# Key norms by products with a block of ones and ln/exp on channels, weight splits with a higher priority, and a new order of the first loads in a hybrid RWKV-7 / FoX block

## The chip, the core and the metric

The kernel runs on one core of a Trainium2 chip. A core has five engines, each with an instruction queue of its own that runs in order: TensorE (PE, matrix products and transposes into PSUM), VectorE (DVE), ScalarE (ACT, functions from tables and copies with a scale), GpSimd (POOL) and SyncE (SP, which here issues nearly all transfers). They wait for each other by semaphores. The metric is the device time of the kernel in microseconds; lower is better.

## The reference

One decoder layer in float32 over 272 tokens (16 meta tokens and 256 of the sequence), model width 2048, 16 heads of 64 in each of two branches, and a SwiGLU FFN of width 5632:

```python
xn = _rms(h, n1)
proj = xn @ w_in
z_rwkv, z_fox, z_gate = jnp.split(proj, (RWKV_COLS, RWKV_COLS + FOX_COLS), axis=-1)
...
# in _rwkv7
kk = heads((k * k_k).astype(F32))
kk = kk / jnp.maximum(jnp.sqrt(jnp.sum(kk * kk, axis=-1, keepdims=True)), 1e-12)
...
# in _fox
q = _rms(q.reshape(B, L, FOX_HEADS, HEAD_DIM), q_g)
k = _rms(k.reshape(B, L, FOX_HEADS, HEAD_DIM), k_g)
...
merged = g_a * (y_a @ w_a) + g_b * (y_b @ w_b)
h = h + merged @ w_o
gate, up = jnp.split(_rms(h, n2) @ w_gu, 2, axis=-1)
return h + (jax.nn.silu(gate) * up) @ w_dn
```

The change bears on the two norms over the 64 channels of a head, that of kk in `_rwkv7` and that of k in `_fox`, and on when things are done, not on what.

## The kernel before

**Layout.** Activations lie with channels on the partitions and tokens along the free dimension (128 x 272). Each large product is made of three float32r products: a weight tile `raw` (128 x 1024 float32) comes by a transfer on SP, ScalarE copies it to `wh` (rounded to float32r, L317), VectorE subtracts to get `wl` (L318), and x is held as the same kind of pair in `xhl`. There are three buffers each of raw, wh and wl. A tile serves one block of 16 to 32 matmuls (some 3 us on TensorE); its buffer is free for the third tile after it when the block's last matmul is done.

**Order of the work.** First come the lora products (`lora_jobs`, tiles `lo`), fed by `raw0` and x in pieces `xs`. The mean square of x is built beside them (`squares`, `rstd1`, tile `rms`), and `lora_post` makes the low rank inputs from them. Then, for each of four groups g of four heads: the products k, v, r and the low rank ones (`rwkv_jobs`), then the fox products q, k, v (`fox_jobs`, all tiles named `f`), then, in groups 0 to 2, two jobs of the gate product (`gate_jobs`, tiles `zg`, 256 columns each; the result of a job is copied out by ScalarE and completed by VectorE in `halves`, L393 and L394, and stored to memory as `zgd`). After group 3 the other gate jobs follow, then the branch products, w_o and the FFN.

**Small work.** What hangs on these products (the WKV recurrence in blocks, `rwkv_bg`; the attention, `fox_bg`; the norms) is written as generators. `slot` is called after every group of three matmuls, adds their time to a clock, and starts the next stage of a generator that is due. A stage yields the time until its next one: these are the constants at the head of the file (NORM, SUMS, Y_KK and the like). TensorE's order is so written out by hand (`manual_schedule`); in the lora part ScalarE's as well. The order on the other queues is made by a scheduler from priorities.

**The head norms before.** `head_sums` multiplies the squares (stationary, 128 channels x up to 128 tokens) with `bsum` (128 x 2), 4-byte float products: the sums of a head come out on token partitions, six products for 272 tokens and two tiles of channels (tiles `ss` for kk, `fss` for q and k). `rsqrt_steps` takes the inverse root there on VectorE with shifts and polynomials, and `spread` brings it back to channels: ScalarE widens it to 128 x 384 (L586) and TensorE transposes it, six transposes (tiles `kx` for kk, `fx` for the fox keys). VectorE multiplies (L679, L991).

**The softmax.** For each pair of heads `fox_bg` makes scores (`sc`), adds the bias of the forget gate with a row maximum, takes Exp on ScalarE with a sum (L1074), divides on VectorE (RECIPROCAL L1077, products L1081, tiles `s`) and transposes on TensorE (tile `ppt`), which ScalarE copies to `pT`; `po` is the product with v. Beside it VectorE runs a long chain of small steps for the inverse of the recurrence's triangular blocks (tiles `lx`, `lt`, L817 and L819).

Of the kernel before, what the change touches and what calls it, by code (L numbers as in the profile page):

```python
# [18 lines left out]
P = 128  # L19
# [47 lines left out]
STEP = 1000  # L67
NORM = 4200
SUMS = 2000
X_RS = 1400  # L70
X_SPREAD = 1400
X_V = 1900
# [4 lines left out]
Y_SQ = 1400  # L77
Y_SPREAD = 3300
Y_KK = 2900
Y_DECAY = 1400  # L80
Y_AB = 4400
Y_MAT = 2900
# [9 lines left out]
Y_GN = 1400  # L92
FORGET = 14000


@with_exitstack
def hybrid_block(ctx, tc, A, out, dbg=None):
# [70 lines left out]
    xh, xl = xhl[:, :, 0, :], xhl[:, :, 1, :]  # L168
    rsb = xp.tile([P, L], F32, tag="rsb", name="rsb")


# [63 lines left out]
    def xsplit(i, m):  # L235

        k, src = 2 * i + m, xs[i][:, m, :]
        nc.scalar.activation(xh[:, k, :], src, AF.Copy, scale=vc("n1", k))
        nc.vector.scalar_tensor_tensor(xl[:, k, :], src, vc("n1", k), xh[:, k, :].bitcast(F32),
                                       op0=ALU.mult, op1=ALU.subtract)  # L240

    def squares(i):

        if i == 0:
            nc.scalar.activation(xsum, xs[i], AF.Square)
# [24 lines left out]
    def rstd1():  # L270
        parts = [et(f"{n}1").bitcast(F32R) for n in ("xqh", "xql")]
        split(*parts, xsum)

        def back():
            ps = aux_ps("rms1")[:, :L]
            for i in range(4):
                nc.tensor.matmul(ps, allones, parts[i % 2][:, i // 2, :], start=i == 0, stop=i == 3)
            ms = zt_("ms1")[:, :L]
            nc.vector.tensor_scalar(ms, ps, 1.0 / D, RMS_EPS, op0=ALU.mult, op1=ALU.add)
            rt = zt_("rt1")[:, :L]  # L280
            rsqrt_small(None, rsb, ms, rt, None)
        return back
# [3 lines left out]

    zw = yb.rearrange("p g t -> p (g t)")[:, :T]
    nc.vector.memset(zw, 0.0)
    pz = aux_ps("warmup")[:, :T]
    for i in range(8):  # L290
        nc.tensor.matmul(pz, zw[:, :P], zw, start=True, stop=True)


    def wload(parts, n, between=None):
# [7 lines left out]
        for prow, c0, shape, srcs in parts:  # L302
# [13 lines left out]
            cs_ = slice(c0, c0 + size)  # L316
            nc.scalar.activation(wh[:prow, cs_], raw[:prow, cs_], AF.Copy)  # L317
            nc.vector.tensor_tensor(wl[:prow, cs_], raw[:prow, cs_], wh[:prow, cs_].bitcast(F32), op=ALU.subtract)  # L318
            res.append((v(wh), v(wl)))
# [152 lines left out]
    def lora_jobs():  # L472
        box = []

        def mk(q):
            def load():
# [18 lines left out]
            def mul(w):  # L495
                if q == 0:
                    box.extend((main_ps if i < 2 else aux_ps)(f"lo{i}") for i in range(4))
                pw, pa, pg0, pg1 = box[:4]
                wh, wl = w
                for k in range(2):  # L500
                    for ps, c0, m, n0, n in ((pw, 0, 96, 0, L), (pa, 96, 112, 0, L),
                                             (pg0, 208, P, 14, T + 2), (pg1, 208 + P, P, 14, T + 2)):
                        kt = q * 2 + k
                        mm3(ps[:m, :n], wh[:, k, c0:c0 + m], wl[:, k, c0:c0 + m],
                            xh[:, kt, n0:n0 + n], xl[:, kt, n0:n0 + n], kt == 0, kt == KT - 1)
# [8 lines left out]
        return [mk(q) for q in range(8)]  # L514

    def lora_post(pw, pa, pg0, pg1):
# [47 lines left out]

    def tiles(n):
        return [(n - T, P), (n - P, P)] + ([(0, NMETA)] if n > T else [])

    def head_sums(dst, sqs, n, name):  # L570


        ps = aux_ps(name)
        if n > T:
            nc.gpsimd.memset(dst, 1.0)
        for i, (t0, w) in enumerate(tiles(n)):
            for m in range(2):
                c = 4 * i + 2 * m
                pe_mm(ps[:w, c:c + 2], sqs[m][:, t0:t0 + w], bsum, start=True, stop=True)
        return [(dst[:w, 4 * i:4 * i + 4], ps[:w, 4 * i:4 * i + 4]) for i, (_, w) in enumerate(tiles(n))]  # L580

    def spread(rs, m, n, name):

        tl = tiles(n)
        ex = et(name).rearrange("p m t -> p (m t)")[:, :3 * P].rearrange("p (i c) -> p i c", c=P)
        nc.scalar.activation(ex[:, :len(tl), :].rearrange("p i (h d) -> p i h d", h=2),  # L586
                             rs.rearrange("p (i m h) -> p i m h", m=2, h=2)[:, :, m, :].unsqueeze(3).to_broadcast(
                                 [P, len(tl), 2, HD]), AF.Copy)

        def back():  # L590
            ps = aux_ps(name)[:, :n]
            for i, (t0, w) in enumerate(tl):
                pe_tr(ps[:, t0:t0 + w], ex[:w, i, :], ident[:w, :w])
            return ps
        return back

# [56 lines left out]
    def rwkv_bg(g, box):  # L653
# [16 lines left out]
        yield Y_SQ  # L670
        kn_ = rw.tile([P, 12], F32, tag="kn", name=f"kn{g}", bufs=2)
        kr_ = rw.tile([P, 12], F32, tag="kn", name=f"kr{g}", bufs=2)
        for d, ps in head_sums(kn_, [sq[:, m, :] for m in range(2)], L, f"ss{g}"):
            nc.vector.tensor_scalar(d, ps, 1e-24, None, op0=ALU.max)
        yield from rsqrt_steps(rw, kr_, kn_, [P, 12], "kt")
        backs = [spread(kr_, m, L, f"kx{g}{m}") for m in range(2)]
        yield Y_SPREAD
        for m in range(2):
            nc.vector.tensor_tensor(kk[:, m, :], kk[:, m, :], backs[m](), op=ALU.mult)  # L679
        yield Y_KK  # L680
# [281 lines left out]
    def fox_jobs(g):  # L962
# [5 lines left out]
        ready = []  # L968
        hs = fx.tile([P, 20], F32, tag="hs", name=f"hs{g}", bufs=4)
        hr = fx.tile([P, 20], F32, tag="hs", name=f"hr{g}", bufs=4)  # L970
        done = []

        def sums(sqs, dst, n):
            c = slice(0, 8) if dst is qn else slice(8, 20)
            for i, (d, ps) in enumerate(head_sums(hs[:, c], sqs, n, f"fss{g}{n}")):
                nc.vector.tensor_scalar(d, ps, 1.0 / HD, eps1[:d.shape[0], i:i + 1], op0=ALU.mult, op1=ALU.add)
            done.append(1)
            return
            yield

        def norms():
            while len(done) < 2:
                yield
            yield from rsqrt_steps(fx, hr, hs, [P, 20], "ht")
            yield X_RS

            nc.vector.tensor_tensor(hs[:, 0:8], hs[:, 0:8], hr[:, 0:8], op=ALU.mult)
            backs = [spread(hr[:, 8:20], m, L, f"fx{g}{m}") for m in range(2)]
            yield X_SPREAD
            for m in range(2):  # L990
                nc.vector.tensor_tensor(kn[:, m, :], kn[:, m, :], backs[m](), op=ALU.mult)  # L991
            yield
            ready.append(1)

        def post(dst, n):
            def f(pss):
                sqs = []
                for m in range(2):
                    ps = pss[m]
                    if dst is vv:  # L1000
                        nc.scalar.activation(dst[:, m, :], ps[:, :n], AF.Copy)
                        continue
                    sq = fx.tile([P, L], F32, tag="sqf", name=f"sqf{g}", bufs=3)
                    if dst is qn:
                        halves(dst[:, m, :], ps)
                        nc.scalar.activation(sq[:, :n], dst[:, m, :], AF.Square)
                    else:
                        nc.scalar.activation(sq[:, :n], ps[:, :n], AF.Square)
                        nc.scalar.activation(dst[:, m, :], ps[:, :n], AF.Copy, scale=qk8)
# [3 lines left out]
                else:  # L1013
                    spawn(sums(sqs, dst, n), SUMS)
                    if dst is kn:
                        spawn(norms(), PREP)
            return f
# [4 lines left out]
    def fox_bg(g, qn, kn, vv, hs, hr, ready):  # L1022
# [12 lines left out]
        yield  # L1035
        while not ready or not gate_done:
            yield X_V
# [72 lines left out]

    with tc.manual_schedule(engines={nc.scalar.engine}):

# [206 lines left out]
def _laid_out(inputs):  # L1319
# [30 lines left out]
    put("n2", a["norm2_g"][0])  # L1350
    return {"hT": hT, "lora": lora, "cols": cols}

# [20 lines left out]
```

## Time and profile before

| | |
|---|---|
| time, median of 3 runs | 1564.14 us (1563.58 to 1564.69) |
| profiled execution | 1564.61 us, of which span 1562.9 us |
| TensorE clock granted | 1.0 throughout |
| busy PE / DVE / ACT / POOL | 1554.3 / 1016.3 / 766.8 / 103.5 us |
| weight splits: wl on VectorE, wh on ScalarE | 605.2 us, 521.3 us (496 each) |
| loads of activation tables on ScalarE | 14, 1.283 us each |
| start of the first lora product, of the first k product | 6.84 us, 32.72 us |

Rows of the timeline give start and length in us, engine, line, operation and "out<-in" by the program's names; in brackets stands how long the engine was idle before and who released it. Rows of the waits give the waiting engine and line, whom it waited for, and the sum, the number and the longest of the waits. A row of windows gives for a stretch the busy time (and number) of PE, PEld, DVE, ACT and POOL, then the granted clock, the share of the DMA engines and GB/s.

### The profile page before, as it was taken

What the parts mean: (1) busy time and instruction counts of PE and PEld (TensorE: products, weight loads), DVE (VectorE), ACT (ScalarE), POOL (GpSimd) and SP (SyncE); (2) the same over time, 40 slices, a digit from 0 to 9 for tenths busy, and PEclk for the clock granted to TensorE, in tenths of its full rate; (3) what the DMA queues carried; (4) which work ended last, traced back from release to release, by engine and by line L of the source; (5) the groups of instructions that cost most, each with busy time, mean ns of one, the idle gap of its engine ahead of it and who ended that gap; (6) DMA issues with size and microseconds to landing.
All of it is one profiled execution on the core that took longest, in us unless ns stands there. A gap on an engine that the chain in (4) does not pass through costs nothing.

```text
span 1562.9 us, 26174 instructions
## 1 busy us (share of the span) xinstructions
PE 1554.3 (99%) x10227; PEld 1366.6 (87%) x10227; DVE 1016.3 (65%) x1854; ACT 766.8 (49%) x1117; POOL 103.5 (7%) x194
## 2 busy tenths in 40 slices
PE   9999999999999999999999999999999999999998
PEld 8999988989889888999888888888888888888887
DVE  8878688677768856875655666566566656444443
ACT  6655455465445544654444554454445544333332
POOL 2121103102203100000000000000000000000000
PEclk9999999999999999999999999999999999999999
DMA  7656546546545566776666666666666666666664
GB/s 238 177 155 173 158 125 180 157 119 168 166 137 146 166 179 190 248 226 225 190 183 181 186 186 190 189 188 188 189 189 188 185 193 187 187 203 198 188 200 131
DMA packets 211483, 283.33 MB, mean 181 GB/s; under 512 B 23888, under 2 KB 128352, under 8 KB 211360
## 3 DMA queue, kind: packets, MB, share of 16 engines
q1 hardware_dynamic: 206752, 277.43, 60.3%
q10 hardware_dynamic: 4608, 4.23, 0.8%
q8 instruction: 80, 1.31, 0.4%
q14 instruction: 43, 0.35, 0.1%
HBM read 274.43 MB, written 7.19 MB: 180 GB/s over the span
## 4 chain that ended last, share of the span: by engine, by line
PE 95%; DVE 2%; DMA 1%; issue 1%; ACT 1%; SPq 0%; ACTq 0%; DVEq 0%; POOL 0%
PE up L387 10%; PE gt L387 10%; PE zg L387 7%; PE dn L1238 5%; PE dn L1237 5%; PE dn L1236 5%; PE up L389 5%; PE gt L389 5%; PE zg L389 3%; PE f L328 2%; PE f L387 2%; PE f L330 2%; PE f L329 2%; PE br L329 2%; PE br L330 2%; PE br L328 2%
## 5 line engine op out<-in xcount | busy, mean ns | idle before, releaser
L318 DVE TENSOR_TENSOR wl<-raw,wh 128x1024 fp32r<-128x1024 f32 (+1 forms) x496 | 605.2, 1221 | 438.7 <-ACT wh L317 437.7
L317 ACT ACTIVATE wh<-raw 128x1024 fp32r<-128x1024 f32 (+1 forms) x496 | 521.3, 1052 | 628.7 <-PE dn L1237 146.3
L387 PE MATMUL gt<-hts,wh 128*128 128x512 f32 x704 | 245.0, 394 | 0.0
L387 PE MATMUL up<-hts,wh 128*128 128x512 f32 x704 | 244.9, 394 | 0.0
L389 PE MATMUL gt<-hts,wl 128*128 128x256 f32 x660 | 186.2, 282 | 0.0
L389 PE MATMUL up<-hts,wl 128*128 128x256 f32 x660 | 186.0, 282 | 0.0
L387 PE MATMUL zg<-xhl,wh 128*128 128x512 f32 x512 | 184.3, 403 | 0.0
L387 PEld LDWEIGHTS up<-hts,wh 128*128 128x128 f32 x704 | 130.1, 188 | 26.5
L387 PEld LDWEIGHTS gt<-hts,wh 128*128 128x128 f32 x704 | 130.1, 188 | 26.4
L1237 PE MATMUL dn<-wh,acl 128*128 128x512 f32 x352 | 139.5, 396 | 0.0
L1236 PE MATMUL dn<-wh,ach 128*128 128x512 f32 x352 | 139.5, 396 | 0.0
L1238 PE MATMUL dn<-wl,ach 128*128 128x512 f32 x352 | 139.5, 396 | 0.0
L389 PE MATMUL zg<-xhl,wl 128*128 128x256 f32 x480 | 135.0, 281 | 0.0
L389 PEld LDWEIGHTS up<-hts,wl 128*128 128x128 f32 x660 | 124.7, 189 | 1.8
L389 PEld LDWEIGHTS gt<-hts,wl 128*128 128x128 f32 x660 | 124.7, 189 | 1.8
L387 PEld LDWEIGHTS zg<-xhl,wh 128*128 128x128 f32 x512 | 94.6, 188 | 20.9 <-issue 1.8
L389 PEld LDWEIGHTS zg<-xhl,wl 128*128 128x128 f32 x480 | 90.6, 189 | 1.1
L1238 PEld LDWEIGHTS dn<-wl,ach 128*128 128x128 f32 x352 | 66.3, 188 | 16.2
L1237 PEld LDWEIGHTS dn<-wh,acl 128*128 128x128 f32 x352 | 66.3, 188 | 16.2
L1236 PEld LDWEIGHTS dn<-wh,ach 128*128 128x128 f32 x352 | 66.3, 188 | 16.1
L328 PE MATMUL f<-xhl,wh 128*128 128x272 f32 x256 | 77.7, 303 | 0.0
L330 PE MATMUL f<-xhl,wl 128*128 128x272 f32 x256 | 73.8, 288 | 0.0
(452 smaller groups left out, 2783.3 us busy)
## 6 DMA issues: line engine op xcount, KB each, us to landing
raw<-in_w_gate_up_dram SPq DMA_DIRECT2D x176, 512.0 KB, 3.8
raw<-in_w_in_dram SPq DMA_DIRECT2D x160, 512.0 KB, 4.1
raw<-in_w_down_dram SPq DMA_DIRECT2D x88, 512.0 KB, 4.7
raw<-in_w_o_dram SPq DMA_DIRECT2D x32, 512.0 KB, 4.3
raw<-in_w_branch_a_dram SPq DMA_DIRECT2D x16, 512.0 KB, 4.4
raw<-in_w_branch_b_dram SPq DMA_DIRECT2D x16, 512.0 KB, 4.8
zgd<-zg ACTq DMA_DIRECT2D x30, 128.0 KB, 2.4
gate<-zgd SPq DMA_DIRECT2D x15, 256.0 KB, 5.6
```

The lines of the kernel that those rows point to most:

```text
L317: nc.scalar.activation(wh[:prow, cs_], raw[:prow, cs_], AF.Copy)
L318: nc.vector.tensor_tensor(wl[:prow, cs_], raw[:prow, cs_], wh[:prow, cs_].bitcast(F32), op=ALU.subtract)
L328: nc.tensor.matmul(ps, wh, ah, start=first, stop=False)
L329: nc.tensor.matmul(ps, wh, al, start=False, stop=False)
L330: nc.tensor.matmul(ps, wl, ah, start=False, stop=last)
L387: nc.tensor.matmul(ps.rearrange("p (a t) -> p a t", a=2), wh, act, start=first, stop=last)
L389: nc.tensor.matmul(ps[:, :T], wl, act[:, 0, :], start=False, stop=False)
L1236: nc.tensor.matmul(box[t], ah[:, kt, ts_], wh[:, k, :], start=first, stop=False)
L1237: nc.tensor.matmul(box[t], al[:, kt, ts_], wh[:, k, :], start=False, stop=False)
L1238: nc.tensor.matmul(box[t], ah[:, kt, ts_], wl[:, k, :], start=False, stop=last)
```

## The change

**Key norms.** kk and the fox keys no longer go over token partitions. `head_norms` splits the squares into a float32r pair and multiplies each half with `bones` (128 x 128, ones in the two blocks of 64): the sum of a head stands at once on each of its channels, over 272 columns; two products for each of two tiles of channels (tiles `ss` and `fk`). The inverse root follows on channels: Ln, then Exp with scale -0.5, then Square on ScalarE, and a correcting step with three operations on VectorE. The query norm stays on token partitions (`q_norms`, 8 columns). The fox keys' root has its tile in the same buffer (tag "bias") as the bias of the attention.

**Splits.** In `wload` both split instructions are issued with a priority that is 200 higher.

**First loads.** The first lora weights come in two pieces at the head of SP's queue, x's first tile with its scale as an extra column on ScalarE's queue, and the other pieces of x one load later than before; the first tile's products run in another order; the warmup shrinks from 8 products of 256 columns to 7 of 128; the mean square of x is used in a stage that is due 2.5 us after the lora products (`token_scales`) rather than at once; VectorE's order too is written by hand in this part. Some of the constants are new.

```diff
-NORM = 4200
-SUMS = 2000
-X_RS = 1400
-X_SPREAD = 1400
+NORM = 6500
+SUMS = 3500
...
+N_SUM = 2000
+N_ROOT = 3600
...
-Y_AB = 4400
+Y_AB = 6000
...
+AHEAD = 200
+SCALES = 2500
...
+    epsw = xp.tile([P, L], F32, tag="epsw", name="epsw")
...
     raw0 = wp.tile([P, 1024], F32, tag="raw", name="raw", bufs=RAWB)
+    x0 = zt_("x0")[:, :L + 1]
     xs[0] = et("xs0")
-    nc.sync.dma_start(xs[0][:, 0], A["hT"][:, 0])
-    nc.scalar.dma_start(raw0[:, :NLO], A["lora"][0][:, :NLO])
+    nc.sync.dma_start(raw0[:, :NLO], A["lora"][0][:, :NLO])
+    nc.scalar.dma_start(x0, A["hT0"])
+    nc.sync.dma_start(raw0[:, NLO:2 * NLO], A["lora"][0][:, NLO:])
+    nc.scalar.dma_start(vcol, A["cols"])
     nc.sync.dma_start(xs[0][:, 1], A["hT"][:, 1])
-    nc.scalar.dma_start(vcol, A["cols"])
-    nc.sync.dma_start(raw0[:, NLO:2 * NLO], A["lora"][0][:, NLO:])
     xload(1)
...
-    zw = yb.rearrange("p g t -> p (g t)")[:, :T]
+    zw = yb.rearrange("p g t -> p (g t)")[:, :P]
...
-    for i in range(8):
-        nc.tensor.matmul(pz, zw[:, :P], zw, start=True, stop=True)
+    for i in range(7):
+        nc.tensor.matmul(pz, zw, zw, start=True, stop=True)
...
-            nc.scalar.activation(wh[:prow, cs_], raw[:prow, cs_], AF.Copy)
-            nc.vector.tensor_tensor(wl[:prow, cs_], raw[:prow, cs_], wh[:prow, cs_].bitcast(F32), op=ALU.subtract)
+            with tc.high_priority(AHEAD):
+                nc.scalar.activation(wh[:prow, cs_], raw[:prow, cs_], AF.Copy)
+                nc.vector.tensor_tensor(wl[:prow, cs_], raw[:prow, cs_], wh[:prow, cs_].bitcast(F32), op=ALU.subtract)
...
-                if q + 2 < 8:
-                    xload(q + 2)
+                if 0 < q < 7:
+                    xload(q + 1)
...
-                    box.pop()()
-                    lora_post(*box)
-                    spawn(forget_gate(), FORGET)
+                    spawn(token_scales(*box), SCALES)
...
+    def head_norms(xs, root, dst, floor, name):
+        parts = []
+        for m in range(2):
+            hi, lo_ = (zt_(f"{n}{name}{m}")[:, :L].bitcast(F32R) for n in ("nh", "nl"))
+            split(hi, lo_, xs[m])
+            parts.append((hi, lo_))
+        yield N_SUM
+        pss = []
+        for m in range(2):
+            ps = aux_ps(f"{name}{m}")[:, :L]
+            for i, part in enumerate(parts[m]):
+                clock[2] += L / 2.4
+                nc.tensor.matmul(ps, bones, part, start=i == 0, stop=i == 1)
+            pss.append(ps)
+        for m in range(2):
+            floor(xs[m], pss[m])
+        ys = root()
+        zs = [zt_(f"nz{name}{m}")[:, :L] for m in range(2)]
+        for m in range(2):
+            nc.scalar.activation(ys[m], xs[m], AF.Ln)
+        for m in range(2):
+            nc.scalar.activation(ys[m], ys[m], AF.Exp, scale=-0.5)
+        for m in range(2):
+            nc.scalar.activation(zs[m], ys[m], AF.Square)
+        yield N_ROOT
+        for m in range(2):
+            nc.vector.tensor_tensor(xs[m], xs[m], zs[m], op=ALU.mult)
+            nc.vector.scalar_tensor_tensor(ys[m], xs[m], -3.0, ys[m], op0=ALU.add, op1=ALU.mult)
+            nc.vector.scalar_tensor_tensor(dst[:, m, :], ys[m], -0.5, dst[:, m, :], op0=ALU.mult, op1=ALU.mult)
...
+        yield from head_norms([sq[:, m, :] for m in range(2)], root, kk,
+                              lambda x_, ps: nc.vector.tensor_scalar(x_, ps, 1e-24, None, op0=ALU.max), f"ss{g}")
...
+        def k_norms(sqs):
+            def root():
+                y = fx.tile([P, 2, L], F32, tag="bias", name=f"fy{g}", bufs=1)
+                return [y[:, m, :] for m in range(2)]
+            yield from head_norms(sqs, root, kn,
+                                  lambda x_, ps: nc.vector.scalar_tensor_tensor(
+                                      x_, ps, 1.0 / HD, epsw, op0=ALU.mult, op1=ALU.add), f"fk{g}")
+            ready.append(1)
...
-    with tc.manual_schedule(engines={nc.scalar.engine}):
+    with tc.manual_schedule(engines={nc.scalar.engine, nc.vector.engine}):
```

The scheduler's order follows, at three places. Lines are those of the kernel in question; in the changed one they are 10 to 28 higher.

VectorE in group 0, at the division of the softmax of the first pair of heads (`s_164` to `s_167` before, `s_165` to `s_168` after; `zg_0_1781` and `zg_0_1768` are the first half of the same gate job). Before:

```order
L1077 RECIPROCAL sums_1848<-sums_1848 128x4
L819 TENSOR_TENSOR lx_1665<-lx_1665,lt_1666 112x6x16
L1081 TENSOR_SCALAR s_164<-s_164,sums_1848 128x144
L817 TENSOR_TENSOR lt_1666<-lx_1665,ln_1476 112x6x15
L1081 TENSOR_SCALAR s_166<-s_166,sums_1848 128x144
L819 TENSOR_TENSOR lx_1665<-lx_1665,lt_1666 112x6x15
L1081 TENSOR_SCALAR s_165<-s_165,sums_1848 128x272
L817 TENSOR_TENSOR lt_1666<-lx_1665,ln_1476 112x6x14
L1081 TENSOR_SCALAR s_167<-s_167,sums_1848 128x272
L819 TENSOR_TENSOR lx_1665<-lx_1665,lt_1666 112x6x14
L394 TENSOR_TENSOR zg<-zg,zg_0_1781 128x256
```

And after:

```order
L328 TENSOR_TENSOR wl<-raw,wh 128x1024
L847 TENSOR_TENSOR lx_1695<-lx_1695,lt_1696 112x7x13
L1100 RECIPROCAL sums_1820<-sums_1820 128x4
L404 TENSOR_TENSOR zg<-zg,zg_0_1768 128x256
L845 TENSOR_TENSOR lt_1696<-lx_1695,ln_1508 112x7x12
L1104 TENSOR_SCALAR s_165<-s_165,sums_1820 128x144
L847 TENSOR_TENSOR lx_1695<-lx_1695,lt_1696 112x7x12
L1104 TENSOR_SCALAR s_167<-s_167,sums_1820 128x144
L845 TENSOR_TENSOR lt_1696<-lx_1695,ln_1508 112x7x11
L1104 TENSOR_SCALAR s_166<-s_166,sums_1820 128x272
L847 TENSOR_TENSOR lx_1695<-lx_1695,lt_1696 112x7x11
L1104 TENSOR_SCALAR s_168<-s_168,sums_1820 128x272
```

The gate's addition moved from behind the four divisions to ahead of the first, and a weight split, which waits for the end of the gate job's third block, to ahead of RECIPROCAL.

ScalarE in group 0, from the end of the first gate job (halves `zg_0` and `zg_1`) to the first exponential. Before:

```order
L317 ACTIVATE wh<-raw 128x1024
L393 ACTIVATE zg<-zg_0_1595 128x256
L317 ACTIVATE wh<-raw 128x1024
L393 ACTIVATE zg<-zg_1_1596 128x256
L1138 DMA zgd<-zg 128x256
L317 ACTIVATE wh<-raw 128x1024
L1138 DMA zgd<-zg 128x256
L317 ACTIVATE wh<-raw 128x1024
L1074 ACTIVATE s_164,sums_1848<-s_164,nm_1855,hr_997 128x144
```

And after:

```order
L830 ACTIVATE BK_1593<-tr_1661 128x2x2x64
L832 ACTIVATE SV_1594<-tr_1661 16x2x2x64
L403 ACTIVATE zg<-zg_0_1587 128x256
L1161 DMA zgd<-zg 128x256
L327 ACTIVATE wh<-raw 128x1024
L403 ACTIVATE zg<-zg_1_1588 128x256
L327 ACTIVATE wh<-raw 128x1024 x2
L1161 DMA zgd<-zg 128x256
L327 ACTIVATE wh<-raw 128x1024
L1097 ACTIVATE s_165,sums_1820<-s_165,nm_1827,hr_1000 128x144
```

The same four splits are in both. The first of them, the one that the next gate job begins with, stood ahead of the copy of `zg_0` and now stands behind it and behind its store.

ScalarE in group 1, between two weight splits, where the fox keys' root is taken. This piece is new (before, two copies of L586 stand there, with no load of a table):

```order
L327 ACTIVATE wh<-raw 128x1024
L618 ACT_TABLE_LOAD
L618 ACTIVATE fy_3124<-sqf_2991 128x272
L620 ACT_TABLE_LOAD
L620 ACTIVATE fy_3124<-fy_3124 128x272
L622 ACTIVATE nzfk_3125<-fy_3124 128x272
L618 ACT_TABLE_LOAD
L618 ACTIVATE fy_3124<-sqf_2994 128x272
L620 ACT_TABLE_LOAD
L620 ACTIVATE fy_3124<-fy_3124 128x272
L327 ACTIVATE wh<-raw 128x1024
L622 ACTIVATE nzfk_3126<-fy_3124 128x272
```

Two channel tiles take Ln and Exp in turn, and a table is loaded ahead of each of the four. In the whole program these loads rise from 14 to 34; TensorE's matmuls fall from 9517 to 9452.

More of the change, by code (lines that the diff above doesn't have):

```diff
@@ L244, in squares @@
         if i == 0:
-            nc.scalar.activation(xsum, xs[i], AF.Square)
+            for m, src in enumerate((x0[:, :L], xs[0][:, 1, :])):
+                nc.scalar.activation(xsum[:, m, :], src, AF.Square)
             return
@@ L563, in forget_gate, with head_sums @@
         gate_done.append(1)
-    def tiles(n):
-        return [(n - T, P), (n - P, P)] + ([(0, NMETA)] if n > T else [])
-    def head_sums(dst, sqs, n, name):
+    def head_sums(dst, sqs, name):
         ps = aux_ps(name)
-        if n > T:
-            nc.gpsimd.memset(dst, 1.0)
-        for i, (t0, w) in enumerate(tiles(n)):
+        for i in range(2):
             for m in range(2):
                 c = 4 * i + 2 * m
-                pe_mm(ps[:w, c:c + 2], sqs[m][:, t0:t0 + w], bsum, start=True, stop=True)
-        return [(dst[:w, 4 * i:4 * i + 4], ps[:w, 4 * i:4 * i + 4]) for i, (_, w) in enumerate(tiles(n))]
@@ L582, in spread @@
[L582 to L595, printed above, removed]
+                pe_mm(ps[:, c:c + 2], sqs[m][:, i * P:(i + 1) * P], bsum, start=True, stop=True)
@@ new lines, in head_sums @@
+        return [(dst[:, 4 * i:4 * i + 4], ps[:, 4 * i:4 * i + 4]) for i in range(2)]
+    def head_norms(xs, root, dst, floor, name):
[27 more added lines that the diff above has]
+            nc.vector.scalar_tensor_tensor(dst[:, m, :], ys[m], -0.5, dst[:, m, :], op0=ALU.mult, op1=ALU.mult)
@@ L670, in rwkv_bg @@
         yield Y_SQ
[L671 to L679, printed above, removed]
+        def root():
+            y = et(f"ny{g}")
+            return [y[:, m, :] for m in range(2)]
+        yield from head_norms([sq[:, m, :] for m in range(2)], root, kk,
+                              lambda x_, ps: nc.vector.tensor_scalar(x_, ps, 1e-24, None, op0=ALU.max), f"ss{g}")
         yield Y_KK
@@ L968, in fox_jobs, with sqf, q_norms, root @@
         ready = []
[L969 to L992, printed above, removed]
+        hs = fx.tile([P, 8], F32, tag="hs", name=f"hs{g}", bufs=4)
+        hr = fx.tile([P, 8], F32, tag="hs", name=f"hr{g}", bufs=4)
+        def sqf(m):
+            return fx.tile([P, L], F32, tag="sqf", name=f"sqf{g}{m}", bufs=3)
+        def q_norms(sqs):
+            for i, (d, ps) in enumerate(head_sums(hs, sqs, f"fss{g}")):
+                nc.vector.tensor_scalar(d, ps, 1.0 / HD, eps1[:, i:i + 1], op0=ALU.mult, op1=ALU.add)
+            yield from rsqrt_steps(fx, hr, hs, [P, 8], "ht")
+            nc.vector.tensor_tensor(hs, hs, hr, op=ALU.mult)
+            ready.append(1)
+        def k_norms(sqs):
+            def root():
+                y = fx.tile([P, 2, L], F32, tag="bias", name=f"fy{g}", bufs=1)
+                return [y[:, m, :] for m in range(2)]
+            yield from head_norms(sqs, root, kn,
+                                  lambda x_, ps: nc.vector.scalar_tensor_tensor(
+                                      x_, ps, 1.0 / HD, epsw, op0=ALU.mult, op1=ALU.add), f"fk{g}")
             ready.append(1)
@@ L1002, in f @@
                         continue
-                    sq = fx.tile([P, L], F32, tag="sqf", name=f"sqf{g}", bufs=3)
+                    sq = sqf(m)
                     if dst is qn:
@@ L1035, in fox_bg @@
         yield
-        while not ready or not gate_done:
+        while len(ready) < 2 or not gate_done:
             yield X_V
```

40 lines of the change are left out of this document (26 added, 14 removed).

## The prediction, made before the changed kernel was run

> **What bounds the kernel now.** I read the page's busy shares and its chain first, then the waits of TensorE, then the timeline at the places that the change touches.
>
> ```profile
> PE 1554.3 (99%) x10227; PEld 1366.6 (87%) x10227; DVE 1016.3 (65%) x1854; ACT 766.8 (49%) x1117; POOL 103.5 (7%) x194
> ...
> PE 95%; DVE 2%; DMA 1%; issue 1%; ACT 1%; SPq 0%; ACTq 0%; DVEq 0%; POOL 0%
> ...
> PE po L350 <- ACT pT L1093: 1.5, 1, 1.5
> PE warmup L291 <- DVE yb L288: 1.2, 1, 1.2
> PE rms L277 <- DVE xql L455: 0.9, 1, 0.9
> PE ppt L354 <- DVE s L1081: 0.6, 2, 0.3
> PE rms L277 <- ACT xqh L454: 0.3, 1, 0.3
> ...
> 45.00:610.00 565.00, 562.93 (x4735) 507.41 (x4734) 421.99 (x1054) 294.01 (x493) 94.66 (x148) 1.00 0.56 158
> ```
>
> TensorE is busy for 99% of the span and its listed waits add up to 4.5 us. So the time falls by what TensorE no longer does, and rises by every wait that it gets; there is little old waiting to win. The last row is the stretch that the change reorders (45 to 610 us; columns PE, PEld, DVE, ACT, POOL): VectorE works 422 of 565 us there, ScalarE 294. They keep up on average; what counts is whether, at one place, their queues hand TensorE its operand late. The sum is made against the profiled execution: 1564.61 us, 1562.9 of it span. The median of the three runs is 1564.14, 0.5 lower, inside their spread.
>
> **TensorE work removed and added.** One group of heads (g = 0) in the timeline of PE:
>
> ```profile
> 77.63 1.15 PE L350 MATMUL ss<-bsum,sq 128*128 128x2 f32 x12
> 78.71 0.50 PE L387 MATMUL f<-xhl,wh 128*128 128x512 f32 x1
> ...
> 85.56 1.07 PE L354 MATMUL kx<-ident,kx 128*128 128x128 f32 x6
> 86.56 0.39 PE L328 MATMUL f<-xhl,wh 128*128 128x272 f32 x1
> ...
> 102.03 1.13 PE L350 MATMUL fss<-bsum,sqf 128*128 128x2 f32 x12
> 103.09 0.39 PE L328 MATMUL f<-xhl,wh 128*128 128x272 f32 x1
> ...
> 115.76 1.07 PE L354 MATMUL fx<-ident,fx 128*128 128x128 f32 x6
> 116.76 0.50 PE L387 MATMUL zg<-xhl,wh 128*128 128x512 f32 x1
> ...
> 111.84 0.28 PE L772 MATMUL bs<-rkh,bones 128*128 128x256 f32 x1
> 112.31 0.29 PE L328 MATMUL f<-xhl,wh 128*128 128x272 f32 x1
> ```
>
> From the start of each piece to the start of what follows: 1.08, 1.00, 1.06 and 1.00 us. The product behind each takes another 0.10 longer than its like (0.50 for the first zg after fx against 0.39, the rate it has elsewhere). That is 4.54 a group, 18.2 for four. In their place come eight float32r products with `bones` a group, 272 columns wide. Four of 256 columns (bs) take 0.47, so four of 272 about 0.50: 1.0 a group, 4.0 in all. Net **-14.2**. The query sums stay.
>
> **The first microseconds.**
>
> ```profile
> 1.24 5.95 PE L291 MATMUL warmup<-yb 128*128 128x256 f32 x16 [1.24 <-DVE yb L288]
> 6.84 0.47 PE L328 MATMUL lo<-xhl,wh 128*96 128x272 f32 x1
> ...
> 30.43 0.28 PE L330 MATMUL lo<-xhl,wl 128*128 128x258 f32 x1
> 32.72 0.29 PE L328 MATMUL k<-xhl,wh 128*128 128x272 f32 x1
> ...
> 3.88 0.67 DVE L487 CAST wh<-raw 128x464 fp32r<-128x464 f32 x1 [2.70 <-DMA raw<-in_lora_dram]
> ...
> 8.52 0.59 ACT L490 ACTIVATE wh<-raw 128x464 fp32r<-128x464 f32 x1 [1.42 <-DMA raw<-in_lora_dram]
> ```
>
> The warmup shrinks to 7 products of half the columns (5.95 x 7/16 = 2.6, done near 3.9), and x comes with its own scale column; what is left is the cast of the first weights, done at 4.55. So the first lora product may start near 4.6 instead of 6.84. The 24 products of its tile take 3 us (0.125 each), and then the second tile is needed, whose split began at 8.52 on a landing. TensorE came there at 9.85; now it waits until about 9.0. I take **-0.9**; the ends are 0 (the landing moves later) and 2.3 (it moves earlier by as much as the first product). The statistics of the first norm (rms) leave the gap ahead of k: 2.29 from the last lora product's start to k's, less 0.12 for that product and 0.5 for the four sums, which stay: **-1.7**; k's first products need weights that are split long before. The two old waits of ppt, 0.6 in the rows above, are within the new ones below and fall as gains: **-0.6**. Gains: 14.2 + 0.9 + 1.7 + 0.6 = 17.4; 20.3 if the landing comes early and the 1.5 of po (a late load) goes as well.
>
> **The softmax transposes (ppt).** Before, VectorE divides s as soon as the sums are there; now a weight split and the gate's addition stand ahead of it.
>
> ```profile
> 139.18 0.60 ACT L1074 ACTIVATE s<-s,nm,hr 128x272 f32<-128x272 f32 x1
> 139.78 1.04 ACT L317 ACTIVATE wh<-raw 128x1024 fp32r<-128x1024 f32 x1
> ...
> 139.91 0.18 DVE L1077 RECIPROCAL sums<-sums 128x4 f32<-128x4 f32 x1
> 140.15 0.29 DVE L1081 TENSOR_SCALAR s<-s,sums 128x144 f32<-128x144 f32 x1
> 140.88 0.36 DVE L1081 TENSOR_SCALAR s<-s,sums 128x272 f32<-128x272 f32 x1
> 142.23 1.23 DVE L318 TENSOR_TENSOR wl<-raw,wh 128x1024 fp32r<-128x1024 f32 x1
> ...
> 139.55 0.39 PE L387 MATMUL zg<-xhl,wh 128*128 128x512 f32 x1
> 139.90 0.40 PE L387 MATMUL zg<-xhl,wh 128*128 128x512 f32 x1
> ```
>
> The split's buffers are freed by the third weight block of the gate product (here the fourth begins at 139.90). From there: wh 1.04 on ScalarE, wl 1.23 on VectorE, then, by the spacing of the rows (139.91 to 140.15 with one lx step between), lx 0.15, RECIPROCAL 0.15, the gate's addition 0.34 (0.42 alone, row below), lt 0.16, the first division 0.29: ready 3.4 after the block's end. TensorE needs only the half block before ppt: four pairs of 0.35 (139.55 to 139.90), 1.4. The operand of the second transposes comes 0.7 behind the first, and their work covers some of it. So at least 2.65 late in each of four groups; behind ppt stand the rest of the gate's block and, on ScalarE, the copies of ppt and of the gate's second half, which come later by as much. With the last exponential, now behind wh (0.60), and one more split (1.23) in the way it would be 4.5. I take 3.2, near the lower end, whose rows are all above: **+12.8** (10.6 to 18).
>
> **The switch from one gate job to the next.** (zg of one column block to zg of the next, one switch in each group.) Before, the next job's first wh is split ahead of the copies of the job that ends (zg halves); now behind the first of them, and in group 0 also behind its store, which waits for VectorE's addition.
>
> ```profile
> 128.91 0.38 ACT L393 ACTIVATE zg<-zg 128x256 f32<-128x256 f32 x1 [3.32 <-PE zg L387]
> 129.19 1.05 ACT L317 ACTIVATE wh<-raw 128x1024 fp32r<-128x1024 f32 x1
> ...
> 129.33 0.42 DVE L394 TENSOR_TENSOR zg<-zg,zg 128x256 f32<-128x256 f32 x1 [1.09 <-ACT zg L393]
> 130.28 1.22 DVE L318 TENSOR_TENSOR wl<-raw,wh 128x1024 fp32r<-128x1024 f32 x1 [0.39 <-ACT wh L317]
> ```
>
> From the first copy: 0.28 to the start of wh, 1.05, 0.05, 1.22 for wl: 2.6, and 0.3 of lx steps; TensorE has 1.4 less 0.15 of other work until the first product with wl. So 1.65 late, and in group 0 (addition 0.42, DMA issue) 2.15: **+7.1** for four. Low end 3.6 (0.9 each, wh alone late), high 8.5.
>
> **ScalarE's tables.** A group had 2 loads of tables and has 7 now; four of them stand in one piece between two weight splits (Ln, Exp, square, Ln, Exp of the fox keys). Before, a load lies between a split and an Ln so:
>
> ```profile
> 54.93 1.06 ACT L317 ACTIVATE wh<-raw 128x1024 fp32r<-128x1024 f32 x1
> 56.01 1.28 ACT L538 ACT_TABLE_LOAD   x1
> 57.30 0.43 ACT L538 ACTIVATE fa<-fa 16x272 f32<-16x272 f32 x1
> ```
>
> Four loads of 1.28 and five operations of 0.43 less what they overlap are some 7.1 us; the next split, and the copies of yT behind it, wait for them. In groups 1 to 3 a transpose (trbk) needs the PSUM of yT: I get 1.1 to 1.85 there, hence **+4.5** (0 if ScalarE comes early, 5.5). Group 0 has no yT. [...]
>
> **Two smaller ones.** In group 0 the bk of mat stands behind a split that waits for a block's end: 1.05 + 1.22 and about 1.6 of bk and its neighbours, less twelve products (1.5): **+2.4** (1.5 to 3). The query sums stand behind a wh: 0.55 once and 0.15 three times, **+1.0** (0 to 1.6). The bk row:
>
> ```profile
> 96.17 0.69 DVE L703 TENSOR_TENSOR bk<-kf,cs 128x512 f32<-128x512 f32 x1
> ```
>
> Queues: on SP the bias loads now wait for the key norm (one buffer for both), with the weight loads of the gate behind them; the loads of X are one weight load further forward. Covered by three raw tiles as far as I can follow, so 0; uncovered it costs the 1.5 of po each time, up to 6.5 in four groups. What comes after the last gate product is the same program in the same order: 0.
>
> Sum: 1564.6 - 17.4 + 12.8 + 7.1 + 4.5 + 2.4 + 1.0 = **1575.0**. With all low ends of the waits (15.7) and the high end of the gains: 1564.6 - 20.3 + 15.7 = 1560.0; with all high ends (36.6) and no gain at the first loads: 1564.6 - 16.5 + 36.6 = 1584.7.
>
> **Rivals.**
> - *The splits are one block further ahead than I read* (faster). There are three buffers of wh and wl. If the split ahead of RECIPROCAL, and the one behind the gate's copies, serve one block later than I take them for, their buffers are free 2.8 us (one block) earlier, more than the 2.65 of ppt and the 1.65 of the switch. Then only the two smaller terms stay: 1564.6 - 17.4 + 3.4 = 1550.6. For it: wh at 129.19 stands behind a copy too, and TensorE does not wait. Against: the waits in the changed program name the third block. 18 in 100.
> - *The loops are half as long*: the engines start up to 0.1 before the end of the last operation, and lateness at one place gives the next a lead. Half of 27.8: 1564.6 - 17.4 + 13.9 = 1561.1. 12 in 100.
> - *Loads late*: SP held by the bias, +6.5 to +8: about 1582. 10 in 100.
> - *A switch of tables costs as much again as its row*: four more of 1.28 in each of three groups, 15.4 us: 1590. Against it stands the Ln that starts 1.29 after its load. 3 in 100. [...]
>
> **How the numbers follow.** Forecast 1575, 57 in 100, its own range 1560 to 1585. About 0.2% (3 us) is what a measurement can tell from no change. Faster: the first rival 18, most of the second 9, and 3 from the forecast's low end: 30. Same: 3 of the second and 4 of the low end: 7. Slower: 63. The range runs from the first rival's 1550.6, rounded down, to late loads with high ends, 1588; outside it I leave half of the first rival, the fourth, and a tail of the third, 17 in 100.
>
> **What would show it.** PE's waits by line: ppt on a division in four groups, 2.6 to 4.5 each; the first zg product of four jobs on wl (or wh), 1.6 to 2.2; trbk in groups 1 to 3 on yT; mat once. ss and fk at 0.5 for four. ScalarE's loads at 1.28 with the next operation directly behind. First lora product near 4.6, no wait of rms. If ppt and zg wait less than 1 us in all, the forecast falls and the time is near 1550. If TensorE's small work costs other than 14.2 less, the first term is wrong.

## The result and the profile after

The changed kernel takes 1592.99 us (median of 4 runs, 1591.42 to 1594.66), the kernel before beside it 1564.41 (4 runs, 1563.58 to 1564.76): ratio 1.0181, 95% interval 1.0169 to 1.0194. It is slower, by 28.6 us. The forecast was slower by 10 and the range ended at 1588: the sign was right, the size wrong. Three executions in the experiments (one each of e1, e2 and e12) took 2496 to 3882 us and are in no median below; the medians of 1562.4 (e1) and 1592.5 (e2) from which later expectations start still count them.

The profiled execution took 1592.48 us, 27.9 more than that of before. First the page, then TensorE's waits (engine, line, whom it waited for; sum, number and longest, us):

```profile
span 1590.8 us, 26044 instructions
...
PE 1551.8 (98%) x10113; PEld 1360.3 (86%) x10113; DVE 1037.7 (65%) x1859; ACT 803.1 (50%) x1186; POOL 91.2 (6%) x186
...
PE 85%; DVE 6%; ACT 2%; DMA 1%; issue 1%; ACTq 0%
...
PE trbk L364 <- ACT ya L970: 8.3, 3, 2.8
PE ppt L364 <- DVE lt L845: 8.2, 3, 2.8
PE zg L399 <- DVE wl L328: 5.7, 5, 1.3
PE ppt L364 <- DVE s L1104: 3.5, 4, 2.7
PE mat L360 <- DVE bk L731: 2.0, 1, 2.0
PE fss L360 <- ACT sqf L1031: 1.5, 1, 1.5
PE v L338 <- DVE fl L546: 1.1, 1, 1.1
...
PE zg L397 <- ACT wh L327: 1.1, 1, 1.1
PE v L338 <- ACT wh L327: 1.0, 1, 1.0
PE ss L611 <- ACT nhss L464: 0.6, 1, 0.6
```

TensorE's part of the chain fell from 95% to 85%, VectorE's rose to 6%. The waits are at ppt, at the first products of zg, at trbk, mat and fss, where the prediction put them, and besides at v and ss, where it did not. The engines' shares hardly moved: VectorE is still at 65%, ScalarE went from 49% to 50%. So no engine became the bound; queues hand things over late at places. The longest of these waits, at ppt in group 2, looks so on VectorE and, last, on TensorE (timeline):

```profile
414.10 1.22 DVE L328 TENSOR_TENSOR wl<-raw,wh 128x1024 fp32r<-128x1024 f32 x1
...
415.40 0.17 DVE L1100 RECIPROCAL sums<-sums 128x4 f32<-128x4 f32 x1
415.49 0.39 DVE L404 TENSOR_TENSOR zg<-zg,zg 128x256 f32<-128x256 f32 x1
...
415.96 0.29 DVE L1104 TENSOR_SCALAR s<-s,sums 128x144 f32<-128x144 f32 x1
...
416.39 1.39 PE L364 MATMUL ppt<-ident,s 128*128 128x128 f32 x4 [2.84 <-DVE lt L845]
```

The weight split and the gate's addition stand ahead of the divisions that ppt needs, as predicted.

Something else is in the windows (stretch, its length, busy time and number of PE, PEld, DVE, ACT, POOL, then the granted clock, DMA share, GB/s):

```profile
413.00:416.00 3.00, 0.55 (x4) 0.23 (x2) 2.86 (x11) 1.04 (x4) 0.72 (x2) 0.96 0.81 237
416.00:418.00 2.00, 1.57 (x6) 1.12 (x7) 1.97 (x10) 0.18 (x1) 2.00 (x2) 0.50 0.68 156
418.00:422.00 4.00, 4.00 (x16) 3.52 (x15) 3.66 (x11) 1.24 (x4) 2.47 (x5) 0.50 0.27 95
422.00:423.00 1.00, 1.00 (x8) 0.57 (x8) 0.84 (x5) 1.00 (x2) 0.00 (x0) 0.71 0.00 0
423.00:426.00 3.00, 3.00 (x31) 2.96 (x28) 2.28 (x8) 0.42 (x2) 0.00 (x0) 1.00 0.24 22
```

From 413.5 TensorE waits 2.84 us for a division. Its granted clock then is 0.50 until 422.6, though it has work again from 416.4. Such spells of half clock, 3.4 or 6.8 us long, follow four of the waits (at 105, 255, 388 and 416 us); one minus the granted clock, summed over windows of 1 us, is 8.5 us in the first 650, and 0 in the kernel before. TensorE sets the end there, so nearly all of these 8.5 us are lost (the first 0.6 us of the last spell still fall into its wait).

### The profile page after: what moved, and what is told of

It is laid out like the page before. It is cut to its first block, busy times and chain, and to the rows that moved or that the text cites. A ratio compares the mean times of both kernels' runs of the same rounds, so it can differ in the third digit from the quotient of the medians.

```text
span 1590.8 us, 26044 instructions
## 1 busy us (share of the span) xinstructions
PE 1551.8 (98%) x10113; PEld 1360.3 (86%) x10113; DVE 1037.7 (65%) x1859; ACT 803.1 (50%) x1186; POOL 91.2 (6%) x186
## 4 chain that ended last, share of the span: by engine, by line
PE 85%; DVE 6%; ACT 2%; DMA 1%; issue 1%; ACTq 0%
PE up L397 10%; PE gt L397 10%; PE zg L397 6%; PE dn L1261 5%; PE dn L1260 5%; PE dn L1259 5%; PE up L399 5%; PE gt L399 5%; PE zg L399 3%; PE br L339 2%; PE br L340 2%; PE br L338 2%; DVE wl L328 2%; PE wo L1260 2%; PE wo L1261 2%; PE wo L1259 2%
## 5 line engine op out<-in xcount | busy, mean ns | idle before, releaser
L397 PE MATMUL zg<-xhl,wh 128*128 128x512 f32 x512 | 189.4, 410 | 1.1 <-ACT wh L327 1.1
```

The lines of the kernel that those rows point to most:

```text
L397: nc.tensor.matmul(ps.rearrange("p (a t) -> p a t", a=2), wh, act, start=first, stop=last)
```

## The experiments

Times are medians; the ratio is to the kernel before, run on the same chip (1564.2 to 1564.4 us). Waits are counted as in the table further down: from a product's start to the next one's start, less the median of its kind. So they come out 0.1 to 0.3 us longer than in the rows of the waits.

**The parts one by one.** First the changed kernel without the priority (e1):

```diff
-            with tc.high_priority(AHEAD):
-                nc.scalar.activation(wh[:prow, cs_], raw[:prow, cs_], AF.Copy)
-                nc.vector.tensor_tensor(wl[:prow, cs_], raw[:prow, cs_], wh[:prow, cs_].bitcast(F32), op=ALU.subtract)
+            nc.scalar.activation(wh[:prow, cs_], raw[:prow, cs_], AF.Copy)
+            nc.vector.tensor_tensor(wl[:prow, cs_], raw[:prow, cs_], wh[:prow, cs_].bitcast(F32), op=ALU.subtract)
```

> The changed kernel without the higher priority of the splits; all else stays. Without it ScalarE takes Ln and Exp of both tiles of channels in turn only once (26 table loads instead of 34) and the gate's addition stands behind the divisions again, but a split still stands ahead of RECIPROCAL. Theory A (the waits come from the order that the priority makes): trbk falls from 2.8 to about 0.3 in three groups (2.56 us of table loads less), ppt by 0.8 to 1 in four, and no half clock behind them: 1593 - 7.5 - 3.6 - 3 = about 1579. Theory B (the waits come from ScalarE's new work for the norms, wherever it stands): within 3 us of 1593.

Measured: 1562.11 us, ratio 0.9989 (0.9979 to 0.9999). More than both theories allowed: without the priority the whole loss is gone. Its waits:

```profile
PE zg L397 <- DVE wl L326: 5.1, 4, 1.3
PE ppt L362 <- DVE s L1102: 1.2, 4, 0.3
...
PE zg L395 <- ACT wh L325: 1.1, 1, 1.1
...
PE fss L358 <- ACT sqf L1029: 0.7, 1, 0.7
PE mat L358 <- DVE bk L729: 0.4, 1, 0.4
...
PE trbk L362 <- ACT ya L968: 0.3, 1, 0.3
```

trbk fell below 0.5, ppt to 0.46 a group, mat and fss to less than half; one spell of half clock is left (1.7 us). The waits of zg at the switch are unchanged: they are not the priority's.

The converse, the kernel before with the priority alone (e2; the same diff the other way on it):

> The kernel before with the higher priority of the splits alone. Theory A: ppt waits 2 to 2.8 us in four groups, as in the changed kernel, since split and gate addition stand ahead of the divisions here too; no other new wait: 1564.4 + 8 to 11 = about 1574. Theory B: the priority moves nothing that TensorE waits for: 1564 to 1566.

Measured: 1591.21 us, ratio 1.0176 (1.0159 to 1.0193). That is 27 us, more than twice what theory A gave, and nearly as much as the whole change. The waits show why:

```profile
PE ss L352 <- ACT sq L671: 8.8, 4, 2.5
PE ppt L356 <- DVE lt L819: 5.9, 3, 2.4
PE ppt L356 <- DVE s L1083: 1.4, 4, 0.4
...
PE mat L352 <- DVE bk L706: 1.2, 1, 1.2
```

ppt waits 8.5 in all, as expected of the sum (with the later divisions; but group 1 has only 0.5 of it). Beside it wait the old sums ss, whose squares now stand behind a split on ScalarE: 9.4 in four groups. Half clock: 10.2. So the same priority harms at other places, depending on what small work is there, and here ScalarE's half of the split does part of the harm.

The norms alone with their delays (e3), and the first loads alone (e4); each is the part of the diff above that its name says.

> The kernel before with the new key norms (and their delays) alone. Gain of TensorE work 14.2. Theory A: the switch of gate jobs waits 1.6 each (its split stands behind the copy here too), mat 2, ppt about 1.5 to 2 each, trbk under 0.5: 1564.4 - 14.2 + 7 + 2 + 7 + 1 = about 1567. Theory B: all the waits of the changed kernel but for those of its start: about 1588.

Measured: 1563.02 us, ratio 0.9990 (0.9981 to 1.0000). The zg waits of the switch are here (7.4), ppt waits 2.0 instead of 7 and mat 0.6 instead of 2. The 14.2 us of TensorE work are won, and 12.5 to 13 are given back: between the two profiles the waits above 0.25 us grow from 3.5 to 14.2, and one spell of half clock costs 1.7. Theory A had the places, and put ppt and mat too high.

> The kernel before with the new first loads and the later use of the mean square alone. Theory A: k starts 2.3 us earlier, and the 2.4 us of new waits within v (on the low rank inputs' work on VectorE and on a split behind it) take it back: 1564.4 within 1. Theory B: the waits within v come from the other parts; the 2.3 us stay: about 1562.

Measured: 1564.22 us, ratio 1.0002 (0.9992 to 1.0011). In the time nothing is left, as theory A said. Its mechanism is there only in part: k starts at 30.72 instead of 32.72 us, but 0.5 of that lead is the four sums of the mean square (rms), which now stand between k's products instead of ahead of them; v waits 0.8 for the low rank inputs, and the wait for a split is not there. In the one profile 0.6 us of the lead is left at the first product of r. That execution (1563.05) is the fastest of the ten, so where the rest goes in the others is not shown.

**Which half of the split.** The changed kernel with the priority on wh alone (e7), and on wl alone (e8):

```diff
             with tc.high_priority(AHEAD):
                 nc.scalar.activation(wh[:prow, cs_], raw[:prow, cs_], AF.Copy)
-                nc.vector.tensor_tensor(wl[:prow, cs_], raw[:prow, cs_], wh[:prow, cs_].bitcast(F32), op=ALU.subtract)
+            nc.vector.tensor_tensor(wl[:prow, cs_], raw[:prow, cs_], wh[:prow, cs_].bitcast(F32), op=ALU.subtract)
```

> The changed kernel with the priority on ScalarE's half of the split (wh) alone. 26 table loads; the gate's addition stands behind the divisions. Theory A (the harm is the place of wl in VectorE's queue): close to the kernel without priority, 1562 to 1566. Theory B (the harm is wh ahead of ScalarE's small work, and of the table loads): over 1580.

> The changed kernel with the priority on VectorE's half of the split (wl) alone. 34 table loads; the gate's addition stands ahead of the divisions. Theory A: ppt waits 2.8 and trbk 2.8 as in the changed kernel, 1588 to 1594. Theory B: under 1570.

Measured: wh alone 1567.09 us (1.0017, 1.0008 to 1.0027), wl alone 1589.38 (1.0161, 1.0145 to 1.0176). Theory A for both, though wh alone lies 1 us above its range: in the changed kernel the place of wl in VectorE's queue makes nearly all of the loss. With wl alone ppt waits 2.5 to 3.0, trbk 2.6 to 2.9, and the half clock costs 10.2. The profiles show the expected order: wl alone brings the 34 table loads and the gate's addition ahead of the divisions, wh alone neither.

**Why trbk.** In the changed kernel a wl stands between the two steps on VectorE that give Ln its input, so Ln, Exp, Ln, Exp alternate. In e10 those steps and both Ln get a still higher priority; the priority of the splits stays:

```diff
-        for m in range(2):
-            floor(xs[m], pss[m])
+        with tc.high_priority(2 * AHEAD):
+            for m in range(2):
+                floor(xs[m], pss[m])
...
-        for m in range(2):
-            nc.scalar.activation(ys[m], xs[m], AF.Ln)
+        with tc.high_priority(2 * AHEAD):
+            for m in range(2):
+                nc.scalar.activation(ys[m], xs[m], AF.Ln)
```

> The changed kernel with the floors and the Ln of both tiles of channels at a still higher priority, so that Ln, Ln, Exp, Exp stand together: 26 table loads instead of 34, the priority of the splits kept. Theory A (the trbk waits are the two more table loads, 2.56 us): trbk falls from 2.9 to about 0.4 in three groups, with two spells of half clock behind it: 1593 - 7.5 - 3.4 = about 1582. Theory B (they are the splits ahead of the copies of yT): 1590 to 1594.

Measured: 1581.93 us (1.0119, 1.0102 to 1.0136), theory A; one wait of trbk is left in the list, 0.2 us. That the sum met the time so well is in part luck: in the profile half clock falls by 1.7 and not by 3.4, since a spell now follows three of the four waits of ppt, and the waits of v fall by 1.5. The piece on ScalarE in group 1 of the changed kernel with what follows it up to trbk, and under it the piece in e10 (timeline):

```profile
241.74 1.06 ACT L327 ACTIVATE wh<-raw 128x1024 fp32r<-128x1024 f32 x1 [1.93 <-PE f L339]
242.82 1.28 ACT L618 ACT_TABLE_LOAD   x1
244.17 0.43 ACT L618 ACTIVATE fy<-sqf 128x272 f32<-128x272 f32 x1
244.61 1.28 ACT L620 ACT_TABLE_LOAD   x1
245.91 0.43 ACT L620 ACTIVATE fy<-fy 128x272 f32<-128x272 f32 x1
246.37 0.43 ACT L622 ACTIVATE nzfk<-fy 128x272 f32<-128x272 f32 x1
246.82 1.28 ACT L618 ACT_TABLE_LOAD   x1
248.11 0.43 ACT L618 ACTIVATE fy<-sqf 128x272 f32<-128x272 f32 x1
248.56 1.28 ACT L620 ACT_TABLE_LOAD   x1
249.86 0.43 ACT L620 ACTIVATE fy<-fy 128x272 f32<-128x272 f32 x1
250.19 1.04 ACT L327 ACTIVATE wh<-raw 128x1024 fp32r<-128x1024 f32 x1
...
251.27 1.23 DVE L328 TENSOR_TENSOR wl<-raw,wh 128x1024 fp32r<-128x1024 f32 x1 [1.84 <-ACT wh L327]
...
253.83 0.86 DVE L972 COPY ya<-yT 64x256 f32<-64x256 f32 x2
...
255.15 1.00 PE L364 MATMUL trbk<-ident,bk 128*128 128x128 f32 x4 [2.72 <-ACT ya L970]
```

```profile
240.49 1.06 ACT L327 ACTIVATE wh<-raw 128x1024 fp32r<-128x1024 f32 x1 [1.93 <-PE f L339]
241.57 1.28 ACT L620 ACT_TABLE_LOAD   x1
242.92 0.78 ACT L620 ACTIVATE fy<-sqf 128x272 f32<-128x272 f32 x2
243.72 1.28 ACT L622 ACT_TABLE_LOAD   x1
245.01 0.75 ACT L622 ACTIVATE fy<-fy 128x272 f32<-128x272 f32 x2
...
246.31 1.04 ACT L327 ACTIVATE wh<-raw 128x1024 fp32r<-128x1024 f32 x1
```

From the table load to the next split it is 7.4 us there and 4.7 here: the two loads of 1.28 that are gone. In these rows each load is followed by its function within 0.1.

**The half clock.** The kernel with the priority alone (e2), with TensorE kept busy in its waits (e9; the added products are read by nothing):

```diff
+    def fill(ps, n):
+        for i in range(n):
+            nc.tensor.matmul(ps[:, :T], bones, xh[:, 0, NMETA:], start=True, stop=True)
...
         ps = aux_ps(name)
+        if name.startswith("ss"):
+            fill(ps, 18)
...
                 ppt = aux_ps(f"ppt{g}{m}{h}")
+                if m == 0 and h == 0:
+                    fill(ppt, 12 if g < 2 else 20)
```

> The kernel with the priority alone, and TensorE kept at work while it waits: 18 products of 256 columns with bones, whose results nothing reads, ahead of ss in each group, 12 or 20 ahead of the first ppt of each group. [...] Theory A (the half clock, 10.2 us lost in the profile of that kernel, follows from TensorE's idle time): the waits keep their ends, the clock stays at 1.0 there: 1592.5 - 8 to 10 = about 1584. Theory B (the clock falls for another reason): 1592 to 1594.

Measured: 1584.56 us (1.0130, 1.0115 to 1.0145), 6.7 us less than e2 (1591.21) with more work on TensorE. That is less than the 10.2 of half clock, and part of it is the filling itself: a product took 0.12 (18 of them 2.28), so where a wait was short (ss in groups 2 and 3, ppt in group 1) the filling is longer than the wait it stands in. Around the first ss, windows of e2 and under them of e9:

```profile
76.00:79.00 3.00, 1.24 (x8) 0.84 (x6) 2.43 (x4) 1.84 (x3) 0.00 (x0) 1.00 0.68 200
81.00:87.00 6.00, 6.00 (x22) 5.16 (x23) 1.83 (x12) 1.29 (x3) 0.11 (x1) 0.50 0.26 82
```

```profile
76.00:79.00 3.00, 3.00 (x23) 2.78 (x22) 2.40 (x4) 1.27 (x2) 0.00 (x0) 1.00 0.68 184
81.00:87.00 6.00, 6.00 (x39) 5.29 (x39) 3.11 (x14) 2.27 (x4) 0.11 (x1) 1.00 0.32 90
```

In the six microseconds behind the wait TensorE does 22 products at a clock of 0.50, and 39 at 1.00 where it was kept busy. No window of e9 up to 600 us shows less than full clock. Theory A, with a smaller gain than it gave.

**The switch, four tries to mend it.** e5, e11 and e12 are without the priority and stand beside e1 (1562.1); e6 keeps it and stands beside the changed kernel. e5 sets three delays as before (`Y_AB = 4400`, `NORM = 4200`, `SUMS = 2000`), e6 does the same, e11 puts a priority of 200 on the loads of raw, e12 sets `N_ROOT = 2800` and `Y_AB = 4900`.

> The changed kernel without the priority and with three delays as before (Y_AB 4400, NORM 4200, SUMS 2000). The first split of the next gate job stands ahead of the copy again. Theory A (the switch waits come from the delays, by which the mat blocks and the loads behind them go one block later): 7.4 us of zg waits go, and what is left of the norms' gain shows: 1562.4 - 7.4 = 1555, down to 1553. Theory B (ScalarE's and VectorE's added work makes these waits, they come back at ss, fk or mat): 1560 to 1563.

> The changed kernel, priority kept, with those three delays as before. The switch is mended here too, the gate's addition stays ahead of the divisions, 32 table loads. Theory A: switch waits of 7.4 go, ppt (13) and the half clock stay: 1593 - 7 = 1586, and not under 1580. Theory B (priority harms only together with the new delays): 1560 to 1568.

> The changed kernel without the priority of the splits, but with a priority of 200 on the loads of raw. At the switch the next job's split stands ahead of the copy in all groups. Theory A: the 7.4 us of zg waits and the 1.7 of half clock behind them go: about 1554. Theory B (loads issued ahead of the small transfers hold those up, and the recurrence behind them): 1562 or more.

> The changed kernel without the priority and with two delays shortened (N_ROOT 2800 instead of 3600, Y_AB 4900 instead of 6000); NORM and SUMS stay. The switch is mended in all groups. Theory A: zg waits of 7.4 and the half clock of 1.7 go, fss and ss stay as they were: about 1554. Theory B (with the shorter delays bk or yT come late, as with the old delays): 1560 to 1570.

Measured: e5 1573.03 us (1.0055, 1.0040 to 1.0070), e6 1592.52 (1.0180, 1.0165 to 1.0195), e11 1568.60 (1.0028, 1.0018 to 1.0038), e12 1572.04 (1.0047, 1.0030 to 1.0063). Each time the wait moved. In e5 the zg waits fell from 7.4 to 4.9, and fss (2.7 in group 0, 1.0 in the others), yT (1.3 to 1.9 in groups 1 to 3) and 5.1 of half clock came. In e11 zg waits no more, and ppt does: 4.7 in group 0, 2.1 to 2.2 in the others. In e6 the waits of trbk went and zg and ppt fell, but fss rose to 9.1 and half clock to 13.7. So theory A holds in none of the three without the priority. Theory B has the direction; only e11 lies in its range, e5 is 10 us above it (the waits came at fss and yT) and e12 2 us above. Of e12 there is no usable profile, so where its 10 us over e1 lie stays open. e6 fits neither theory. No version clearly beats the kernel before: the best are e1, 2.1 us below it with an interval that ends at 0.9999, and e3, 1.2 us below.

## Why the prediction fell short

Predicted terms, and what the profile after shows at the same places (us):

| | predicted | measured |
|---|---|---|
| TensorE work of the norms | -14.2 | -14.2 |
| end of the lora products | -0.9 | -0.2 |
| gap between them and k | -1.7 | -1.7 |
| old waits of ppt and po | -0.6 | -2.5 |
| ppt, four groups | +12.8 | +13.2 |
| switch of gate jobs | +7.1 | +7.4 |
| trbk, groups 1 to 3 | +4.5 | +8.8 |
| mat, group 0 | +2.4 | +2.2 |
| fss | +1.0 | +1.7 |
| v, a split and the low rank inputs | 0 | +2.4 |
| ss (1.1), a zg job at 573 us (0.8) | 0 | +1.9 |
| half clock | 0 | +8.5 |
| sum | +10.4 | +27.5 |

The sum of the measured terms leaves 0.4 of the 27.9.

- **The places and mechanisms were right where they were named.** ppt, switch and mat came within 0.5 us of their terms; the products with `bones` take 0.286 alone and 0.5 for four, as the bs rows said. What was not separated was their source: in the changed kernel nearly all of ppt, trbk and mat comes from the priority of wl (e1, e7, e8), and the switch from the norms with their delays (e3). Three delays set back took only 2.5 of the switch's 7.4 away (e5), so how much of it is the delays is not shown.
- **The largest missing term is the half clock.** The step that failed is to price a wait by its own length alone. That a wait can also halve TensorE's clock for 3.4 or 6.8 us afterwards, no row of before shows: its longest listed wait is 1.5 us, its granted clock 1.0 throughout. In the changed kernel it followed waits listed at 2.0 to 2.8 us. Put at nothing in the prediction, half clock was 8.5 of the 17.5 us that its sum lacks; that it follows from TensorE's idle time e2 and e9 show (10.2 us with the waits, none up to 600 us where TensorE was kept busy in them).
- **trbk was taken at half its size.** The piece on ScalarE was right (7.1 predicted, 7.4 from load to split). What was too short is the way from it to the copies of yT: behind the next split (1.04) stand its wl (1.23) and the three last steps of the key norm (1.4) on VectorE, in front of VectorE's two copies, with ScalarE's last copy behind them. The term names the split and the copies; its 1.1 to 1.85 is not worked out, so which of these steps it lacks is inferred from the rows. e10 took 2.6 of ScalarE's piece away and nearly all of the wait with it.
- **The start was not a gain.** k starts 2.3 us earlier, which is near the predicted 2.6 by luck. The first lora product came where it was expected (4.71, predicted near 4.6) and the second tile 1.3 earlier, but waits on that tile and the next ones used the lead up: the last lora product starts 0.15 earlier, not 0.9. The gap behind it closed as predicted, and another 0.5 of k's lead is only the four sums of the mean square, which moved in between k's products. k's first products do find their weights, as predicted; the step that failed is to look no further than k. v waits 1.3 for the low rank inputs, which come later with the later mean square (0.8 in e4), and 1.2 for a wh, a wait that no other run shows above 0.4. e4 alone gives 0.
- **The rivals.** The splits were not one block further ahead, the loops not half as long, table loads cost their row only (1.283 us each, the next function 0.01 to 0.07 behind, once 0.26). TensorE's list has no wait for late loads; the old wait of po, which that rival was priced by, even went.

## What to carry to other kernels

Price a new wait of TensorE by its length and by what follows it: in the changed kernel four of eight waits of 2 us or more cost another 1.7 to 3.4 us at half clock. A blanket priority for the long operations of a queue puts them ahead of the short ones that TensorE waits for next; in e2 VectorE was at 65% and ScalarE at 48%, and the change of order alone cost 27 us. And taking 14 us off the busiest engine moved the waits here rather than the end: see first which wait is next at each place.

## What the runs showed of the hardware

- In the changed kernel four of eight waits of TensorE listed at 2.0 to 2.8 us, among them one of four at ppt, were followed by a granted clock of 0.50: at 105, 255 and 388 us for 3.4 us (cost 1.7 each), at 416 us for 6.8 us (cost 3.4). The waits of ppt that end at 151, 284 and 550 us (2.68 each) and that of trbk at 523 us (2.79) were not. In e1, where no listed wait is longer than 1.3 us, it came too, at 132 us (cost 1.7), behind 4 us in which TensorE was busy for 1.9. What decides is not shown.
- Kept busy in its waits by products that nobody reads, TensorE kept a clock of 1.00 in every window up to 600 us (e9); with the same priority and without them, half clock cost 10.2 us (e2).
- A table load takes 1.283 us, in all 14 of the kernel before and all 34 of the changed one. In the latter the next function starts 0.01 to 0.07 us behind the load (once, 0.26), and what stands ahead of it ends 0.02 before.
